# A hybrid mLSTM, Hyena and mixture-of-experts block on one core: its output projection in two passes, one half's chunks moved forward, and ring slots laid out anew

## The chip, the cores and the metric

The kernel runs on one core of one Trainium2 chip. The metric is the device time of one launch in microseconds (us). Before the change the median of three runs is 1379.07 us (1377.23 to 1380.62). The profiled execution, from which all rows below come, took 1378.79 us; its trace spans 1377.1 us.

## The reference

One encoder block on a sequence of 512 tokens, 1024 channels, in float32.

```
mod = c @ W_ada + b_ada                       # shift, scale, gate, twice
p   = (rms_norm(x) * (1 + sc1) + sh1) @ W_in  # q, k, v, o (4 heads x 128), gates, x1, x2, v of hyena
y_m = mlstm(q, k, v, o, gates)                # 4 heads, forward and backward, 512 channels
y_h = hyena(x1, x2, v)                        # 512 channels, two long convolutions by FFT
x   = x + gt1 * (concat(y_m, y_h) @ W_out)
hf  = rms_norm(x) * (1 + sc2) + sh2
aff = softmax(hf @ w_router)                  # 16 experts
g, idx = top_k(aff.T, 64)                     # each expert takes its 64 best tokens
x   = x + gt2 * sum over experts of silu(xs @ w_gate) * (xs @ w_up) @ w_down * g
out = rms_norm(x)
```

The weights of the experts are 16 x 3 matrices of 1024 x 2048 floats, 403 MB in all.

## The kernel before

**Stages.** First come the adaptive modulation (`w,par` matmuls on `in_w_ada`) and the spectra of Hyena's filters (`filters`, with DFT matmuls `s,d` on TensorE and complex products `H`, `j`, `k` on VectorE). Then `ORDER` lists the input projection in 512-channel parts and what follows each: `Z`, `X1`, `X2` are Hyena's parts, `C0` and `C1` its two long convolutions' forward sides, `I0` and `I1` the inverse ones, `K`, `Q`, `V`, `G`, `O` the mLSTM's parts, `H0` to `H3` its heads. The last large matmuls of this stage are those of `O`.

**Heads.** `stage(h, rows)` computes one head: four score matmuls (`x,y`), after each of which ScalarE and VectorE make weights `pt`; then `weighted` forms 20 sums (`j,pt`, 128x129) for the two directions. `head_out(h)` transposes the result and splits it into a high and a low part, the two halves `s` of `mixT[h]`. `cm_row` fetches a row for a head with a DMA on ScalarE's queue. `mixT[4]` to `mixT[7]` are Hyena's four chunks.

**Output projection.** `out_proj(i, q)` makes a tile of 128 tokens by 512 channels: 24 matmuls of 128x512 (8 chunks of three), Hyena's chunks first, then one VectorE multiply by `gt1` and one add into the residual `xt`. Eight such tiles are made in the order of `STEPS`. In this stage TensorE's order is pinned to program order (`pinned[0]`). Every finished tile starts a `turned` generator: transposes, the router's product, then, in `affinity`, the softmax, and at token tiles 1 and 3 `top64` (8 `MAX` and 7 `MATCH_REPLACE` on VectorE). `FOLLOW` says at which chunk of later tiles the generators take their next step.

**Weight ring.** The experts' matrices are read in 192 tiles of 2 MB on the SP queue, in order, into a ring of 8 slots. The ring's memory overlays that of the mixers, so each of its first 8 tiles waits until the mixer's slots under it are free. `SLOTS` gives the number of buffers of each tag.

VectorE, ScalarE and SP each run their instructions strictly in order. Elsewhere than in the pinned stage the order of an engine is that of the scheduler that builds the program.

## Time and profile before

| what | value |
|---|---|
| median of 3 runs | 1379.07 us (1377.23 to 1380.62) |
| profiled execution, its span | 1378.79 us, 1377.1 us |
| TensorE (PE) busy | 1277.3 us, 93% of the span |
| VectorE (DVE) busy | 514.8 us, 37% |
| ScalarE (ACT) busy | 259.4 us, 19% |
| read from memory | 460.53 MB, 338 GB/s over the span |

Times in rows are counted from the span's start. A row of the timeline gives the start, the duration, the engine and line, the operation with its output and input names, the shape and how many records are grouped. A float32 matmul that is no transpose shows as two records, one of kind fp32r and a transpose as one. The idle time ahead of an instruction and what ended it stand in brackets.

### The profile page before, as it was taken

To read this page: it belongs to the slowest core of one execution; us is meant where nothing else is said; L and a number is where in the kernel's file an instruction comes from. 1 tells how busy PE (TensorE), PEld (TensorE's weight loads), DVE (VectorE), ACT (ScalarE), POOL (GpSimd) and SP (SyncE) were. 2 spreads that over 40 slices of the span, in tenths; PEclk is the share of its full clock that TensorE was granted. 3 is DMA by queue.
4 is the path that set the end of the run, shared out by engine and by line. 5 is a ranking of instruction groups with operands and counts; after the bars stand their busy time and mean duration, and the time that the engine had idled before them with its cause. 6 is when DMAs were issued, how large, how long until landed. Compare 5 with 4: busy or idle time off the path is not lost.

```text
span 1377.1 us, 14496 instructions
## 1 busy us (share of the span) xinstructions
PE 1277.3 (93%) x5845; PEld 594.7 (43%) x5845; DVE 514.8 (37%) x1057; ACT 259.4 (19%) x561; POOL 32.4 (2%) x72
## 2 busy tenths in 40 slices
PE   4999999997896999999989998998999899899896
PEld 1466686674773334334333432433343243234332
DVE  5866796797663122221212212122121122212131
ACT  4523321456330101001010100101011010000111
POOL 0000000000000000000000000000000000000000
PEclk9999999999997999999999999999999999999999
DMA  9544444644109999999999999999999999999995
GB/s 350 181 169 140 151 154 136 198 144 169 61 20 408 393 430 425 427 426 427 428 426 426 426 425 427 430 426 425 427 425 427 428 426 426 427 426 427 428 406 214
DMA packets 58258, 466.06 MB, mean 338 GB/s; under 512 B 5448, under 2 KB 20040, under 8 KB 32464
## 3 DMA queue, kind: packets, MB, share of 16 engines
q1 hardware_dynamic: 53632, 455.56, 80.9%
q10 hardware_dynamic: 3216, 5.65, 1.3%
q0 software_dynamic: 1344, 3.94, 0.8%
q8 instruction: 46, 0.75, 0.2%
q14 instruction: 20, 0.16, 0.0%
HBM read 460.53 MB, written 4.60 MB: 338 GB/s over the span
## 4 chain that ended last, share of the span: by engine, by line
PE 72%; DMA 20%; DVE 3%; ACT 2%; issue 2%; POOLq 0%; SPq 0%; POOL 0%; DVEq 0%; ACTq 0%
PE ps L176 68%; DMA r<-in_w_up_dram 17%; PE ps L236 4%; DMA out_dram<-a 2%; DMA b<-in_hy_w_dram 1%; DMA w<-in_w_ada_dram 1%; DMA M<-cmd 1%; DVE M L1233 0%; ACT I L1232 0%; DVE M L990 0%; DVE M L992 0%; ACT jk L834 0%; ACT H L847 0%; ACT ps L268 0%; DVE a L1125 0%
## 5 line engine op out<-in xcount | busy, mean ns | idle before, releaser
L176 PE MATMUL ps<-r,x 128*64 128x512 f32 x2048 | 507.7, 616 | 34.0 <-DMA r<-in_w_up_dram 26.6
L176 PEld LDWEIGHTS ps<-r,x 128*64 128x64 f32 x2048 | 142.2, 140 | 305.6 <-issue 253.4
L176 PE MATMUL ps<-r,M 128*64 128x512 f32 x1024 | 232.0, 598 | 7.4 <-DVE M L1233 6.8
L1182 DVE SCALAR_TENSOR_TENSOR a<-ps,aff,a 128x512 f32<-128x512 f32 x120 | 90.1, 751 | 164.3 <-PE ps L176 164.3
L176 PEld LDWEIGHTS ps<-r,M 128*64 128x64 f32 x1024 | 69.3, 136 | 130.8 <-issue 118.0
L1222 DVE COPY I<-ps 128x512 f32<-128x512 f32 x32 | 22.1, 692 | 238.2 <-PE ps L176 222.1
L1224 ACT COPY I<-ps 128x512 f32<-128x512 f32 x32 | 18.7, 585 | 486.5 <-PE ps L176 486.5
L176 PE MATMUL ps<-a,l 128*128 128x512 f32 (+1 forms) x200 | 83.7, 418 | 0.0
L176 PE MATMUL ps<-a,h 128*128 128x512 f32 x192 | 81.0, 422 | 0.0
L1233 DVE TENSOR_TENSOR M<-ps,I 128x256 f32<-128x256 f32 x64 | 27.2, 424 | 141.4 <-ACT I L1232 139.7
L176 PE MATMUL ps<-b,h 128*128 128x512 f32 x192 | 79.9, 416 | 0.0
L176 PEld LDWEIGHTS ps<-M,h 128*128 128x128 f32 x512 | 63.3, 198 | 24.3 <-issue 17.0
L176 PE MATMUL ps<-M,h 128*128 128x128 f32 x512 | 68.9, 289 | 1.4 <-DVE M L1192 1.4
L176 PEld LDWEIGHTS ps<-V,H 128*128 128x128 f32 x120 | 22.3, 186 | 97.4 <-DVE a L1182 78.7
L176 PE MATMUL ps<-V,H 128*128 128x512 f32 x120 | 59.6, 497 | 0.0
L176 PE MATMUL ps<-s,d 128*128 128x512 f32 x112 | 56.5, 602 | 0.2 <-ACT H L361 0.2
L1232 ACT ACTIVATE I<-ps 128x256 f32<-128x256 f32 x64 | 24.5, 383 | 164.9 <-PE ps L236 164.9
L236 PEld LDWEIGHTS ps<-par,I 128*128 128x128 f32 x268 | 36.3, 208 | 40.8 <-issue 38.7
L1257 DVE TENSOR_TENSOR H<-ps,gt 128x512 f32<-128x512 f32 x15 | 10.4, 691 | 102.9 <-PE ps L176 102.9
L236 PE MATMUL ps<-par,I 128*128 128x128 f32 x268 | 45.8, 302 | 1.7 <-DVE I L1222 1.7
L176 PEld LDWEIGHTS ps<-a,h 128*128 128x128 f32 x192 | 36.1, 188 | 18.9 <-issue 9.6
L240 DVE TENSOR_TENSOR l<-w,h 128x1024 fp32r<-128x1024 f32 x32 | 38.1, 1219 | 16.4 <-ACT h L239 13.9
(313 smaller groups left out, 1148.9 us busy)
## 6 DMA issues: line engine op xcount, KB each, us to landing
r<-in_w_gate_dram SPq DMA_DIRECT2D x63, 2048.0 KB, 28.0
r<-in_w_up_dram SPq DMA_DIRECT2D x63, 2048.0 KB, 31.8
...
a<-in_w_ada_dram SPq DMA_DIRECT2D x2, 1024.0 KB, 15.1
...
```

What stands on the lines that cost most here:

```text
L176: return pin(pe.matmul(o, l, r, start=start, stop=stop))
L236: pin(pe.transpose(o, i, ident[0:k, 0:k]))
L240: dve.tensor_tensor(lo, v, hi.bitcast(F32), op=OP.subtract)
L1182: dve.scalar_tensor_tensor(xs, ps, aff[:, i, e:e + 1], xs, op0=OP.mult, op1=OP.add)
L1222: dve.tensor_copy(gs, gu[j])
L1224: act.copy(gs, gu[j])
L1232: act.activation(sg, pv[:, :, 0, :], AF.Silu)
L1233: dve.tensor_tensor(hidT[j // 2][:, j % 2 * 4:j % 2 * 4 + 4, :], pv[:, :, 1, :], sg, op=OP.mult)
L1257: dve.tensor_tensor(y, dn, gt2, op=OP.mult)
```

## The change

It does five things. `SLOTS` gives two of the four `s` buffers a tag `t` of their own, which the filters' sums, the spectra and Hyena's finished chunks use; the filter weights `w3` come in two halves, and four loads of `in_w_ada` go to other slots. `ORDER` puts `X1`, `I0` ahead of `K`, and `H0`, `H1` behind `I1`; `H3` is no longer in it. `out_proj` takes a list of chunks: it is called for chunks 4 to 7 of all eight tiles, and later for chunks 0 to 3 of all eight, and each call ends with the multiply and the add. The last head's `stage` yields after each score matmul and each `weighted`, and `WEAVE` takes its six pieces in between the eight first-pass tiles. `STEPS` has another order, and `FOLLOW` counts chunks over all tiles.

```diff
-SLOTS = {"h": 2, "a": 2, "x": 1, "l": 2, "s": 4, "j": 1, "k": 2, "b": 2, "y": 1, "d": 1}
+SLOTS = {"h": 2, "a": 2, "x": 1, "l": 2, "s": 2, "t": 2, "j": 1, "k": 2, "b": 2, "y": 1, "d": 1}
-ORDER = "Z C0 K Q X1 G I0 V C1 H0 H1 X2 I1 H2 O H3".split()
+ORDER = "Z C0 X1 I0 K C1 Q G V X2 I1 H0 H1 H2 O".split()
-STEPS = ((0, 0), (1, 0), (0, 1), (1, 1), (2, 0), (2, 1), (3, 0), (3, 1))
+STEPS = ((0, 0), (0, 1), (1, 0), (1, 1), (2, 0), (2, 1), (3, 0), (3, 1))
+WEAVE = (1, 1, 0, 0, 0, 1, 0, 1, 0, 1, 0, 1, 1, 1)
-FOLLOW = (3, 3, 5, 8, 1)
+FOLLOW = (3, 6, 8, 15, 16)
...
-            w3 = slot8("b")
-            for q in range(2):
-                sp.dma_start(w3[64 * q:64 * q + 64, :], a["hy_w3"][0])
+            w3 = [half(), half()]
+            for n in (1, 0):
+                for q in range(2):
+                    sp.dma_start(w3[n][64 * q:64 * q + 64, :], a["hy_w3"][0][:, n * 1024:(n + 1) * 1024])
...
-                plus, minus = q4(slot8("s")), q4(slot8("s"))
+                plus, minus = q4(slot8("t")), q4(slot8("t"))
...
-                    w = slot8("ab"[k // 2 % 2])
+                    w = slot8("ajak"[k // 2])
...
-            mixh, mixl = slot8("s", F32R), slot8("s", F32R)
+            mixh, mixl = slot8("t", F32R), slot8("t", F32R)
...
-        for q, g, t0 in ((0, 1, "h"), (0, 0, "h"), (1, 1, "x"), (1, 0, "y")):
+        for q, g, t0 in ((0, 1, "h"), (1, 1, "b"), (0, 0, "h"), (1, 0, "y")):
             wh = q4(slot8(t0, F32R))
-            wl = q4(slot8("jd"[g] if q else "l", F32R))
+            wl = q4(slot8("db"[g] if q else "l", F32R))
...
-        def out_proj(i, q):
+        def out_proj(i, q, ks):
+
             ps = bank("P")
             cs_ = slice(q * 512, (q + 1) * 512)
-            for n, k in enumerate((4, 5, 6, 7, 0, 1, 2, 3)):
-                yield n
-                mm3(ps, [t[:, i * 128:(i + 1) * 128] for t in mixT[k]], wo[q, k], start=(k == 4), stop=(k == 3))
+            for k in ks:
+                yield k
+                mm3(ps, [t[:, i * 128:(i + 1) * 128] for t in mixT[k]], wo[q, k], start=(k == ks[0]), stop=(k == ks[-1]))
...
-        early = [out_proj(*st) for st in STEPS[:EARLY]]
-        for g in early:
-            for n in g:
-                if n == 4:
-                    break
+
+        last_head = stage(3, [cm_row(6 + d) for d in range(2)])
+        hyenas = [out_proj(i, q, (4, 5, 6, 7)) for i, q in sorted(STEPS, key=lambda st: st[1])]
+        for n in WEAVE:
+            if n:
+                for _ in hyenas.pop(0):
+                    pass
+            else:
+                next(last_head)
         for h in range(3):
             head_out(h)
-        for g in early:
+        early = [out_proj(*st, (0, 1, 2, 3)) for st in STEPS[:EARLY]]
+        for m, g in enumerate(early):
+            if m == EARLY - 1:
+                head_out(3)
             for n in g:
-                if n == 7:
+                if n == 3:
                     break
-        head_out(3)
         for m, st in enumerate(STEPS):
-            for n in [7] if m < EARLY else out_proj(*st):
+            for n in [3] if m < EARLY else out_proj(*st, (0, 1, 2, 3)):
                 for t in todo:
-                    if t[1] and t[1][0] == n:
+                    if t[1] and t[1][0] <= 4 * m + n:
                         t[1].pop(0)
                         next(t[0], None)
...
-            todo.append((turned(*st), list(FOLLOW)))
+            todo.append((turned(*st), [4 * m + 4 + n for n in FOLLOW]))
```

**Place one: TensorE and VectorE behind the last DFT matmul of the filters.** Rows of the built program, with line, operation, output and input. On TensorE of the kernel before, behind the last `s,d` matmul, transposes of a first convolved part `V_650` stand ahead of 24 matmuls of the next part, and those of `V_686` and `V_749` behind them:

```order
L176 MATMUL ps_584<-s_481,d_81 128x512
L236 MATMUL ps_655<-par,V_650 128x128 x4
L176 MATMUL ps_949<-a_346,h_697 128x512
L176 MATMUL ps_949<-b_348,h_697 128x512
L176 MATMUL ps_949<-a_346,l_698 128x512
...
L236 MATMUL ps_691<-par,V_686 128x128 x4
L236 MATMUL ps_754<-par,V_749 128x128 x4
```

In the changed kernel the last DFT matmul is `t_484,d_84`, and the same transposes follow it (`V_653`, `V_689`, `V_752`):

```order
L178 MATMUL ps_587<-t_484,d_84 128x512
L178 MATMUL ps_710<-w_1002,par 32x512 x2
L178 MATMUL ps_710<-w_1003,par 32x512 x2
L239 MATMUL ps_658<-par,V_653 128x128 x4
L239 MATMUL ps_694<-par,V_689 128x128 x4
L239 MATMUL ps_757<-par,V_752 128x128 x4
L178 MATMUL ps_956<-a_349,h_700 128x512
```

The 24 projection matmuls now come behind the third group of transposes. On VectorE of the changed kernel this stands between that DFT matmul's result (`ps_587`) and `V_752`:

```order
L371 SCALAR_TENSOR_TENSOR H_593<-ps_587,H_591 128x512
L371 SCALAR_TENSOR_TENSOR H_591<-ps_587,H_591 128x512
L378 TENSOR_TENSOR j_544<-H_593,H_575 128x512 x2
L378 TENSOR_TENSOR j_544<-H_591,H_566 128x512 x2
L569 TENSOR_TENSOR V_752<-V_752,ecol 128x2
L569 TENSOR_TENSOR V_788<-V_788,ecol 128x2
L570 SCALAR_TENSOR_TENSOR V_752<-ps_727,vcol,V_752 128x511
L570 SCALAR_TENSOR_TENSOR V_788<-ps_763,vcol,V_788 128x511
L571 SCALAR_TENSOR_TENSOR V_752<-ps_727,vcol,V_752 128x511
```

In the kernel before these rows are the same, without the two of the second part (`V_788`) and with one of another part among them.

**Place two: TensorE between the last matmul of `O` and the first of the output projection.** Before, Hyena's transposes (`par,s`) and head 3 stand there:

```order
L236 MATMUL ps_2408<-par,s_2122 128x128 x4
L236 MATMUL ps_2417<-par,s_2122 128x128 x4
L176 MATMUL ps_2736<-j_1528,pt_2696 128x129 x3
L176 MATMUL ps_2741<-j_1528,pt_2696 128x129 x4
L176 MATMUL ps_2753<-j_1528,pt_2697 128x129 x4
L176 MATMUL ps_2759<-j_1528,pt_2697 128x129 x3
L176 MATMUL ps_2764<-j_1528,pt_2697 128x129 x2
L176 MATMUL ps_2768<-j_1528,pt_2697 128x129
L176 MATMUL ps_2807<-par,mod_598 128x16 x8
L176 MATMUL ps_2880<-h_2819,s_2388 128x512
```

In the changed kernel Hyena's transposes are followed by the last sums of head 1 (`pt_2324`) and then by all of head 2, and `h,t` is the first matmul of the projection:

```order
L239 MATMUL ps_2175<-par,s_1889 128x128 x4
L239 MATMUL ps_2184<-par,s_1889 128x128 x4
L178 MATMUL ps_2391<-j_1638,pt_2324 128x129 x2
L178 MATMUL ps_2395<-j_1638,pt_2324 128x129
L178 MATMUL ps_2443<-x_1378,y_1098 128x512
...
L178 MATMUL ps_2466<-x_1378,y_1098 128x512
L178 MATMUL ps_2474<-j_1638,pt_2441 128x129
...
L178 MATMUL ps_2513<-j_1638,pt_2442 128x129
L239 MATMUL ps_2571<-par,I_2565 128x128 x4
L178 MATMUL ps_2692<-par,mod_601 128x16 x8
L178 MATMUL ps_2777<-h_2704,t_2155 128x512
```

Head 3's four scores and 20 sums have moved from here into the first pass.

**Place three: VectorE at the end of the output projection.** `H_3327` (before) and `H_3334` (changed) are the product of the last tile with `gt1`; `MAX` of 16 rows is the first `top64`. Before, that `top64` ends ahead of the last tile's product:

```order
L990 MAX M_2878<-M_2878 16x8
L958 COPY M_2878<-M_2878 16x64
L971 SCALAR_TENSOR_TENSOR lg_3310<-ps_2877,rq_3293,lb 128x16
L973 TENSOR_REDUCE mx_3312<-lg_3310 128x1
L976 RECIPROCAL mx_3313<-mx_3313 128x1
L977 TENSOR_SCALAR aff<-aff,mx_3313 128x16
L907 TENSOR_TENSOR H_3327<-ps_3261,I_2864 128x512
...
L908 TENSOR_TENSOR a_2861<-a_2861,H_3327 128x512
...
L935 COPY V_3344<-ps_3339 128x256
...
L971 SCALAR_TENSOR_TENSOR lg_3370<-ps_2877,rq_3353,lb 128x16
```

In the changed kernel six of its seven `MATCH_REPLACE` stand behind the last tile's sum `a_2746`, and the copy `V_3379` and the logits `lg_3405` of the last token tile wait in line behind them:

```order
L916 TENSOR_TENSOR a_2746<-a_2746,H_3334 128x512
L981 TENSOR_REDUCE mx_3359<-lg_3357 128x1
L1000 MATCH_REPLACE M_2763<-M_2763 16x256
L998 MAX M_2763<-M_2763 16x8
...
L1000 MATCH_REPLACE M_2763<-M_2763 16x256
L943 COPY V_3379<-ps_3374 128x256
L998 MAX M_2763<-M_2763 16x8
L966 COPY M_2763<-M_2763 16x64
L979 SCALAR_TENSOR_TENSOR lg_3405<-ps_2762,rq_3388,lb 128x16
```

The first `top64` has moved from ahead of the last tile to behind it.

## Rows read from the trace of the kernel before

**Rows 1.** Busy time by stage (windows): window, its length, busy us (and instructions) of PE, PEld, DVE, ACT, POOL, the granted clock of TensorE, DMA share and GB/s.

```profile
100.00:150.00 50.00, 50.00 (x204) 31.58 (x203) 28.88 (x45) 19.05 (x27) 0.00 (x0) 1.00 0.47 148
316.99:351.30 34.31, 24.38 (x138) 17.40 (x136) 26.88 (x83) 25.69 (x87) 1.78 (x4) 0.90 0.38 139
351.30:409.98 58.68, 54.53 (x294) 42.32 (x294) 35.28 (x111) 17.70 (x45) 0.00 (x0) 1.00 0.10 37
409.98:427.87 17.89, 5.68 (x30) 4.78 (x29) 12.77 (x57) 2.75 (x7) 0.00 (x0) 0.58 0.97 392
478.00:1355.00 877.00, 839.17 (x3787) 315.16 (x3786) 192.43 (x334) 85.98 (x180) 13.46 (x33) 0.98 1.01 426
```

**Rows 2.** Timeline of TensorE around the last DFT matmul of the filters.

```profile
113.01 1.05 PE L176 MATMUL ps<-w,par 128*32 128x512 f32 x4
114.00 1.12 PE L176 MATMUL ps<-s,d 128*128 128x512 f32 x2
114.96 0.63 PE L236 MATMUL ps<-par,V 128*128 128x128 f32 x4
...
121.00 1.12 PE L236 MATMUL ps<-par,V 128*128 128x128 f32 x8
```

**Rows 3.** Timeline of VectorE in the same stretch.

```profile
115.24 0.69 DVE L367 SCALAR_TENSOR_TENSOR H<-ps,H 128x512 f32<-128x512 f32 x1 [0.92 <-PE ps L176]
...
117.04 1.28 DVE L374 TENSOR_TENSOR j<-H,H 128x512 f32<-128x512 f32 x2
...
118.32 1.28 DVE L374 TENSOR_TENSOR j<-H,H 128x512 f32<-128x512 f32 x2
...
120.30 0.75 DVE L567 SCALAR_TENSOR_TENSOR V<-ps,vcol,V 128x511 f32<-128x511 f32 x1
```

**Rows 4.** Timeline of TensorE from the last matmul of `O` (the first row) past the first (351.30) and the last matmul (409.59) of the output projection to the first expert's gather (427.87).

```profile
316.99 0.80 PE L176 MATMUL ps<-a,l 128*128 128x512 f32 x1
...
322.58 3.96 PE L176 MATMUL ps<-j,pt 128*128 128x129 f32 x34
...
326.87 2.74 PE L176 MATMUL ps<-x,y 128*128 128x512 f32 x6
337.45 2.49 PE L236 MATMUL ps<-par,s 128*128 128x128 f32 x8 [7.85 <-DVE s L838]
...
342.04 1.04 PE L236 MATMUL ps<-par,s 128*128 128x128 f32 x8
...
349.59 1.85 PE L176 MATMUL ps<-par,mod 128*128 128x16 f32 x16
351.30 0.48 PE L176 MATMUL ps<-h,s 128*128 128x512 f32 x1
...
359.40 0.39 PE L176 MATMUL ps<-x,s 128*128 128x512 f32 x1
...
409.59 0.39 PE L176 MATMUL ps<-y,s 128*128 128x512 f32 x1
...
427.87 0.58 PE L176 MATMUL ps<-M,h 128*128 128x128 f32 x1 [1.41 <-DVE M L1192]
```

**Rows 5.** Instructions grouped by line and shape, 317.6 to 428 us: line, engine, operation, out<-in, shapes, count, busy us, mean ns, idle before them.

```profile
L240 DVE TENSOR_TENSOR l<-w,h 128x1024 fp32r<-128x1024 f32 x2 | 2.4, 1217 | 0.0
...
L838 DVE TENSOR_TENSOR s<-s,zrs 128x512 f32<-128x512 f32 x4 | 2.5, 686 | 0.0
...
L848 DVE CAST s<-H 128x512 fp32r<-128x512 f32 x4 | 1.7, 424 | 0.7 <-ACT H L847 0.7
...
L907 DVE TENSOR_TENSOR H<-ps,I 128x512 f32<-128x512 f32 x8 | 5.5, 690 | 2.3 <-PE ps L176 2.2
```

**Rows 6.** Timeline of VectorE from the first `top64` to the last token tile's probabilities.

```profile
397.65 0.42 DVE L990 MAX8 M<-M 16x8 f32<-16x256 f32 x1
...
398.18 0.40 DVE L992 MATCH_REPLACE8 M<-M 16x256 f32<-16x256 f32 x1
...
407.84 0.42 DVE L990 MAX8 M<-M 16x8 f32<-16x256 f32 x1
...
415.03 0.23 DVE L971 SCALAR_TENSOR_TENSOR lg<-ps,rq,lb 128x16 f32<-128x16 f32 x1
...
416.62 0.23 DVE L977 TENSOR_SCALAR aff<-aff,mx 128x16 f32<-128x16 f32 x1
```

**Rows 7.** Timeline of the SP queue: issues of ring tiles.

```profile
321.00 0.46 SPq L1093 DMA_DIRECT2D r<-in_w_gate_dram  x1
370.38 0.34 SPq L1093 DMA_DIRECT2D r<-in_w_up_dram  x1
409.82 0.33 SPq L1093 DMA_DIRECT2D r<-in_w_gate_dram  x1
...
412.26 0.48 SPq L1093 DMA_DIRECT2D r<-in_w_up_dram  x1
440.91 11.45 SPq L1093 DMA_DIRECT2D r<-in_w_down_dram  x4
```

**Rows 8.** Windows of ten microseconds in the first expert; columns as in rows 1.

```profile
437.00:447.00 10.00, 9.22 (x47) 3.98 (x48) 0.18 (x1) 0.46 (x1) 0.00 (x0) 1.00 0.92 349
477.00:487.00 10.00, 10.00 (x52) 4.04 (x50) 0.85 (x2) 1.35 (x3) 0.00 (x0) 1.00 1.02 431
```

**Rows 9.** What TensorE waited for between 478 and 1355 us: us in all, times, the longest.

```profile
PE ps L176 <- DMA r<-in_w_up_dram: 26.6, 11, 3.8
```

More of the change, by code (lines that the diff above doesn't have):

```diff
@@ L305, in body @@
                 dve.tensor_tensor(hidp[lo, c], hid[hi, :], hidp[hi, c].bitcast(F32), op=OP.subtract)
-            w3h, w3l = slot8("s", F32R), slot8("l", F32R)
+            w3l, w3h = slot8("l", F32R), slot8("s", F32R)
             for b in (2, 3, 0, 1):
                 bs = slice(b * 512, (b + 1) * 512)
+                w = w3[b // 2][:, b % 2 * 512:b % 2 * 512 + 512]
                 with tc.issue_after(sins[W3A]):
-                    act.copy(w3h[:, bs], w3[:, bs])
-                dve.tensor_tensor(w3l[:, bs], w3[:, bs], w3h[:, bs].bitcast(F32), op=OP.subtract)
+                    act.copy(w3h[:, bs], w)
+                dve.tensor_tensor(w3l[:, bs], w, w3h[:, bs].bitcast(F32), op=OP.subtract)
         sel4 = slot8("h", F32R)
@@ L768, in stage @@
                     dve.scalar_tensor_tensor(v, ps[:, rg], SCALE, v, op0=OP.mult, op1=OP.mult)
+                yield
             for d in range(2):
                 weighted(h, d, pts[d])
+                yield
         def weighted(h, d, pt):
@@ L807, in head @@
         def head(h):
-            stage(h, [cm_row(2 * h + d) for d in range(2)])
+            for _ in stage(h, [cm_row(2 * h + d) for d in range(2)]):
+                pass
         def gated_1():
@@ L1021, in body @@
                 next(early[m], None)
-            for t in todo:
-                if t[1] and t[1][0] == 8 and m >= EARLY:
-                    t[1].pop(0)
-            todo.append((turned(*st), list(FOLLOW)))
+            todo.append((turned(*st), [4 * m + 4 + n for n in FOLLOW]))
         if dbg:
```

3 lines of the change are left out of this document (2 added, 1 removed).

## The prediction

> **What bounds the kernel now.** I read the stages first [rows 1]. From 478 to 1355 us the weights stream at 426 GB/s with a DMA share of 1.01, and TensorE waits there for arriving tiles, 26.6 us in all for one of the three matrices [rows 9]: the experts are a DMA stream. One tile of 2.097 MB takes 4.92 us at that rate. How that stream starts comes next [rows 7]. Two ring tiles are issued early, six in a row from 409.82 to 412.26, and the ninth only at 440.91, when TensorE frees a slot; around then the rate sinks to 349 GB/s and is back at 431 forty us later [rows 8]. So the ring is full before the first expert begins, and what starts the stream again is TensorE's work in that expert. The end of the kernel therefore follows the start of the first expert, 427.87 us [rows 4], nearly one for one. Ahead of that TensorE is the bound: between 100 and 150 us it is busy 50.00 of 50 [rows 1], so a hole made there lengthens the kernel. Only after the last matmul of the projection `O` (T0 = 316.99) is it idle: 9.9 of 34.3 us until the output projection starts at 351.30, 4.2 of 58.7 until the end of its last matmul, which starts at 409.59, and 12.2 of 17.9 until the gather [rows 1, 4].
>
> **How I worked.** I laid the instructions of the changed kernel, in the order of each engine, against durations from rows of before: each starts when the one ahead of it on its engine and the one it waits for are done. Prices on TensorE: a projection matmul 0.231 us (36 from 351.30 to 359.40), a weighted sum `j,pt` 0.233 (17 in 3.96), a score `x,y` 0.91 (3 in 2.74), a transpose 0.13 (8 in 1.04), a DFT matmul 0.96 (114.00 to 114.96) and a `w,par` matmul 0.5 (two from 113.01 to 114.00) [rows 2, 4]. On VectorE: 0.69 for 512 floats with about 0.08 of it overlapped, 0.42 for a cast, 1.22 for a split of a weight half [rows 5]. The same walk over the old order gives 32.2, 58.3 and 18.9 us for the three stretches where the trace has 34.3, 58.3 and 18.3, which is my measure of its error.
>
> **Before T0: +4.3 us.** By count, 17 weighted sums and 3 scores move from ahead of T0 to behind it and 4 DFT matmuls come ahead of it: -4.0 - 2.7 + 3.8 = -2.9 us. Against that stands a new hole at place one. Before, 5.5 us of projection matmuls lie between the transposes at 114.96 and those at 121.00, while VectorE works from 115.24 to 121.05 through two `H`, four `j` and two steps of `V` [rows 2, 3]. After, the transposes of the same `V` come right away: TensorE has four `w,par` matmuls (1.9 us) and eight transposes (1.0) beside a chain on VectorE of 6.1 + 0.7 us, since one step of the next part stands inside it too. The hole is 6.8 - 2.9 = 3.9 us. Smaller holes come out at the start of the first projection (a PSUM bank that VectorE frees, about 0.9) and at three later places (0.7 to 1.0 each); I take 3.3 for all, with 0 and 5 as ends. The sum is +4.3. The halved `w3`, the four moved loads and the tag `t` cost nothing: they lie in the start-up, which waits for other things; without that cover a load of 0.5 MB costs 1.2 us at 426 GB/s.
>
> **T0 to the first projection matmul: 34.3 becomes 26.7.** VectorE is what TensorE waits for. Behind T0 it still has four products with `zrs` (2.4, of which 0.9 lie ahead of T0), four weight splits (4.6), eight casts and subtractions of Hyena's halves (3.8), three steps of head 1 (1.9), seven pieces of `pt` (2.8), `k` and small ones (2.0): 16.6 us until the bank of head 2's last score is free, 16.2 in the walk. Then TensorE does that score, 20 sums, four transposes and the modulation's products (1.85): 8.0, and 1.5 of waits for ScalarE's copies; 25.7 in all. Before, the 7.85 us wait at 337.45 was followed by slow work: eight transposes took 2.49 us, at 342.04 again 1.04, and the clock granted over the whole stretch was 0.90 [rows 1, 4]. After, there is a wait of about 5.7 us ahead of that last score. I add 1.0 us for work at the lower clock (ends 0 and 2.3). Gain: 7.6 us.
>
> **The two passes: 58.3 becomes 66.9.** The 192 matmuls stay: 44.4 us. Head 3 has come in: four scores 3.6 and 20 sums 4.7, so pass one lasts 22.2 + 8.3 + 1.5 (12 transposes) = 32.0. At the seam the first `s` halves wait for VectorE and ScalarE as before, 0.3 us more. The eight additional products and sums are 16 x 0.69 = 11 us on VectorE; they cost nothing, since pass one gives it 32 us for some 25 us of work, and would cost a bank wait of 0.7 us each without that. Loss: 8.6 us.
>
> **The end: 18.3 becomes 23.6.** Before, the first `top64` ran from 397.65 to 408.26, ahead of the last matmul, and the last token's probabilities came at 416.62 [rows 6]. `FOLLOW` now lets token tile 1 finish at step 4 x 3 + 4 + 16 = 32, and the last step is 31, so the first `MAX` starts some 1.2 us ahead of the last matmul. What VectorE must do until the last token's logits is 8 x 0.45 + 7 x 0.52 us of `top64` and 5 us of other steps in line, 12.2 in all, which ends 11.0 us behind the last matmul; the softmax takes 1.3 more. The probabilities come 12.3 us after it, not 7.0 (409.59 to 416.62). Queued behind are the second `top64`, the slots and the gather. Loss: 5.3 us, nearly sure, as VectorE runs in order.
>
> **The ring: -1 us.** Five tiles instead of two can load before the last matmul: the second slot is freed by the last matmul of pass one, three by `head_out(3)`. But the ring was already full when the first expert began to free slots; by 477 us some 0.2 of a tile more has landed: 1.0 us. The far end is three tiles, 14.7 us.
>
> **Sum:** 4.3 - 7.6 + 8.6 + 5.3 - 1.0 = +9.6. On the profiled execution's 1378.79 us, 0.28 below the median, that gives 1388.4 us.
>
> **The rivals.** *The weave fills the idle time.* From T0 to the last matmul TensorE is busy 24.4 + 54.5 = 78.9 of 93.0 us [rows 1]. If pass one starts as soon as Hyena's halves are there and the sums of head 3 fill every hole, 14.1 us go instead of the 1.0 that I add there: 1388.4 - 15.1 = 1373.3 us. For it: the holes are real, and VectorE is idle in the middle of them. Against it: all of head 2 stands ahead of pass one in TensorE's order (place two), and its last score waits for VectorE. It decides at a start of pass one about 13 us behind T0, where the walk has those halves ready. Chance 0.13. The Trainium skill, "Perfetto Trace Analysis", section Optimization Strategy, says that a kernel whose most contended engine changes over time may be improved by interleaving those regimes; that is what the weave is, and by it this rival would be the likeliest; the trace agrees with its premise by the idle 14.1 us, and no run here shows yet what follows from it.
>
> *The ring's start sets the end.* Then three tiles more ahead of the experts take 14.7 us off instead of 1: 1374.7, not slower. For it: the share is 1.01 from 478 on. Against it: the dip to 349 GB/s and the issue at 440.91, which waits for TensorE [rows 7, 8]. It would need slots freed before the first expert runs. Chance 0.04.
>
> *The late terms cancel.* If the hole at place one is covered (VectorE further ahead than in the trace) and the smaller ones as well, 4 to 7 us go; if the last token's logits were not held up, 5.3. One gives 1381 to 1384, both 1376 to 1379: no measurable change. Chance 0.16.
>
> *More half-clock work.* If the wait ahead of pass one puts its first 30 matmuls at the lower clock, they take 7 us more: above 1394. Against it: only 1.5 us of waiting directly precede them. Chance 0.06.
>
> **The numbers.** Chances: forecast, 1383 to 1394, 0.61; the rivals 0.13, 0.04, 0.16, 0.06. A measurement of this kernel tells about 0.3%, 4 us, from no change: slower is above 1383.2, faster below 1374.9. So slower 0.67, same 0.16, faster 0.17. The range reaches down to about the first two rivals' times and up to the end of the forecast's, 1374 to 1394; what it leaves out is the fourth rival and the better half of the first. The forecast's own range is 1383 to 1394.
>
> **What would show it.** A hole of about 4 us on TensorE near 119, ended by a step of `V` on VectorE; T0 near 321; the first `h,t` matmul about 27 us later; the last `y,s` near 415; no 16x256 `MAX` more than 2 us ahead of it; the probabilities some 12 us behind; the gather near 438; five ring tiles issued before the last matmul, and a rate of 0 GB/s for a while between the eighth tile's landing and the first freed slot. I am wrong if the hole near 119 is missing, if pass one starts within 20 us of T0, or if the end doesn't follow the gather.

## The result and the profile after

The changed kernel takes 1392.35 us (median of 4 runs, 1391.20 to 1394.16) beside 1379.82 us before on the same chip: a ratio of 1.0098 with a 95% interval of 1.0086 to 1.0109. It is slower: the medians are 12.5 us apart, and by the ratio it is 13.5. The forecast was 1388.4 us, and slower. The profiled execution took 1394.16 us with a span of 1392.5, 15.4 us more span than before. Where they went is read at the same places as before:

| us, profiled executions | before | forecast | after |
|---|---|---|---|
| first matmul of `Z` | 73.13 | no change | 75.97 (+2.8) |
| last matmul of `O` (T0) | 316.99 | +4.3 | 325.60 (+8.6) |
| T0 to first projection matmul | 34.3 | 26.7 | 26.6 (-7.7) |
| first to last projection matmul | 58.3 | 66.9 | 66.7 (+8.4) |
| last projection matmul to gather | 18.3 | 23.6 | 24.6 (+6.3) |
| gather to the end of the span | 949.2 | -1.0 | 949.0 (-0.2) |

The rows of after that answer to [rows 1], in the same columns; the first is a stretch of the start-up and has its row of before right behind it.

```profile
30.00:40.00 10.00, 7.71 (x31) 2.32 (x34) 6.14 (x10) 1.33 (x2) 0.00 (x0) 0.83 0.85 313
100.00:150.00 50.00, 46.09 (x189) 31.17 (x188) 23.71 (x35) 14.46 (x20) 0.00 (x0) 0.97 0.32 103
325.60:352.20 26.60, 19.41 (x122) 15.97 (x121) 20.16 (x56) 16.87 (x48) 1.82 (x4) 0.81 0.35 112
352.20:418.88 66.68, 62.03 (x339) 47.75 (x339) 45.49 (x126) 26.66 (x76) 1.27 (x2) 1.00 0.43 165
418.88:443.46 24.58, 7.44 (x32) 6.16 (x31) 19.99 (x84) 4.53 (x11) 0.00 (x0) 0.58 0.64 256
```

```profile
30.00:40.00 10.00, 10.00 (x42) 3.00 (x41) 7.29 (x13) 2.31 (x4) 0.00 (x0) 1.00 0.94 356
```

TensorE was busy all of 30 to 40 us and all of 100 to 150 us before; after, it lacks 2.29 us in the one and 3.91 in the other. The stretch of the two passes is well filled (62.0 of 66.7), the tail behind it is not (7.4 of 24.6). The timeline of TensorE of after names the waits; the bracket gives the idle time ahead of a row and what ended it.

```profile
33.52 2.28 PE L178 MATMUL ps<-w,par 128*32 128x512 f32 x6 [2.29 <-DMA w<-in_w_ada_dram]
...
75.97 0.50 PE L178 MATMUL ps<-a,h 128*128 128x512 f32 x1 [1.08 <-DVE M L406]
...
116.43 1.30 PE L239 MATMUL ps<-par,V 128*128 128x128 f32 x8
121.65 0.72 PE L239 MATMUL ps<-par,V 128*128 128x128 f32 x4 [3.92 <-DVE V L571]
122.12 0.67 PE L178 MATMUL ps<-a,h 128*128 128x512 f32 x1
...
125.58 0.44 PE L178 MATMUL ps<-a,l 128*128 128x512 f32 x1
...
341.85 2.08 PE L178 MATMUL ps<-x,y 128*128 128x512 f32 x2 [6.67 <-DVE pt L772]
...
432.58 0.38 PE L239 MATMUL ps<-par,aff 128*16 128x128 f32 x1 [1.43 <-DVE aff L985]
439.86 0.26 PE L239 MATMUL ps<-par,mx 16*128 16x16 f32 x1 [6.89 <-DVE mx L1050]
...
443.46 2.08 PE L178 MATMUL ps<-M,h 128*128 128x128 f32 x8 [1.41 <-DVE M L1203]
```

And the SP queue of after, which answers to [rows 7]: the second pair of `w` tiles of `w_ada` and the two pairs behind it in the start-up, then the first and the fifth tile of the ring.

```profile
17.17 19.85 SPq L439 DMA_DIRECT2D w<-in_w_ada_dram  x6
...
368.50 0.34 SPq L1104 DMA_DIRECT2D r<-in_w_gate_dram  x1
...
392.72 0.42 SPq L1104 DMA_DIRECT2D r<-in_w_gate_dram  x1
```

### The profile page after: what moved, and what is told of

Same layout as the page of the kernel before. It is cut to its first block, busy times and chain, and to the rows that moved or that the text cites. A ratio compares the mean times of both kernels' runs of the same rounds, so it can differ in the third digit from the quotient of the medians.

```text
span 1392.5 us, 14525 instructions
## 1 busy us (share of the span) xinstructions
PE 1279.6 (92%) x5845; PEld 608.3 (44%) x5845; DVE 524.0 (38%) x1073; ACT 260.9 (19%) x561; POOL 29.9 (2%) x72
## 4 chain that ended last, share of the span: by engine, by line
PE 73%; DMA 19%; DVE 4%; issue 2%; ACT 1%; SPq 0%; POOLq 0%; POOL 0%; ACTq 0%; DVEq 0%
PE ps L178 70%; DMA r<-in_w_up_dram 14%; PE ps L239 4%; DMA w<-in_w_ada_dram 2%; DMA out_dram<-a 2%; DMA M<-cmd 1%; DMA w<-in_hy_w_dram 1%; DVE M L1000 0%; DVE M L1244 0%; DVE M L998 0%; ACT I L1243 0%; DVE a L1136 0%; DVE H L915 0%; DVE a L916 0%; DVE H L371 0%
## 5 line engine op out<-in xcount | busy, mean ns | idle before, releaser
L178 PEld LDWEIGHTS ps<-r,x 128*64 128x64 f32 x2048 | 152.3, 139 | 294.2 <-issue 229.7
L178 PEld LDWEIGHTS ps<-r,M 128*64 128x64 f32 x1024 | 69.5, 136 | 132.1 <-issue 119.5
L1233 DVE COPY I<-ps 128x512 f32<-128x512 f32 x32 | 22.1, 691 | 242.5 <-PE ps L178 226.3
L178 PEld LDWEIGHTS ps<-M,h 128*128 128x128 f32 x512 | 63.3, 198 | 24.3 <-issue 17.0
L1243 ACT ACTIVATE I<-ps 128x256 f32<-128x256 f32 x64 | 24.5, 383 | 164.9 <-PE ps L239 164.9
L1118 DVE TENSOR_SCALAR x<-ps,A,mod 128x128 f32<-128x128 f32 x32 | 13.1, 410 | 94.2 <-PE ps L178 94.2
L178 PE MATMUL ps<-w,par 128*32 128x512 f32 x160 | 33.7, 650 | 15.2 <-ACT ps L271 9.3
L243 DVE TENSOR_TENSOR l<-w,h 128x1024 fp32r<-128x1024 f32 x32 | 38.4, 1219 | 17.0 <-ACT h L242 15.4
```

Of the source, the lines that this page charges most:

```text
L178: return pin(pe.matmul(o, l, r, start=start, stop=stop))
L243: dve.tensor_tensor(lo, v, hi.bitcast(F32), op=OP.subtract)
L1118: dve.tensor_scalar(xsT[:, k, :], v, A2[:, k:k + 1], mod2[:, 0, k:k + 1], op0=OP.mult, op1=OP.add)
L1233: dve.tensor_copy(gs, gu[j])
L1243: act.activation(sg, pv[:, :, 0, :], AF.Silu)
```

## The experiments

Twelve kernels were run. The times are compared as ratios to the kernel before on the same chip, with 95% intervals; the places come from each one's timeline (one profiled execution each, in us; T0 is the last matmul of `O`, P the projection's matmuls).

| kernel | first `Z` | T0 | T0 to first P | first to last P | last P to gather | gather to end | ratio |
|---|---|---|---|---|---|---|---|
| before | 73.13 | 316.99 | 34.3 | 58.3 | 18.3 | 949.2 | 1 |
| after | 75.97 | 325.60 | 26.6 | 66.7 | 24.6 | 949.0 | 1.0098 (1.0086 to 1.0109) |
| e_w3 | 73.61 | 323.80 | 23.8 | 68.1 | 24.6 | 949.0 | 1.0083 (1.0065 to 1.0100) |
| e_ordc | 75.81 | 327.36 | 26.1 | 68.3 | 24.3 | 949.5 | 1.0138 (1.0116 to 1.0161) |
| e_order | 75.70 | 322.41 | 26.1 | 69.7 | 24.6 | 948.8 | 1.0099 (1.0082 to 1.0117) |
| e_tag | 75.28 | 327.64 | 24.5 | 66.7 | 24.6 | 948.2 | 1.0102 (1.0084 to 1.0120) |
| e_ordtt | 74.53 | 318.65 | 23.0 | 69.5 | 24.3 | 950.6 | 1.0070 (1.0058 to 1.0082) |
| e_both | 76.67 | 330.03 | 12.7 | 77.1 | 24.0 | 948.6 | 1.0066 (1.0051 to 1.0081) |
| e_top1 | 76.95 | 328.15 | 24.0 | 68.3 | 22.1 | 950.0 | 1.0078 (1.0061 to 1.0095) |
| b_pass | 73.77 | 317.63 | 22.2 | 69.9 | 24.0 | 947.7 | 1.0045 (1.0030 to 1.0060) |
| e_onepass | 75.18 | 325.09 | 39.8 | 58.4 | 18.3 | 948.2 | 1.0101 (1.0086 to 1.0115) |
| e_slots | 76.48 | 326.65 | 24.2 | 68.5 | 24.6 | 948.5 | 1.0102 (1.0087 to 1.0118) |
| e_best | 73.69 | 317.29 | 19.2 | 75.8 | 19.8 | 948.3 | 1.0027 (1.0018 to 1.0036) |
| b_slots | 72.62 | 316.48 | 27.9 | 58.4 | 18.3 | 950.1 | 0.9963 (0.9949 to 0.9977) |

A place in one execution is no median. After, e_onepass and e_top1 have the same code ahead of T0, and T0 lies at 325.60, 325.09 and 328.15, so a difference of 3 us there tells nothing by itself.

### The halves of the change: b_pass and e_onepass

**The passes alone.** From the changed kernel, everything ahead of the projection goes back to what it was:

```diff
-ORDER = "Z C0 X1 I0 K C1 Q G V X2 I1 H0 H1 H2 O".split()
+ORDER = "Z C0 K Q X1 G I0 V C1 H0 H1 X2 I1 H2 O".split()
...
-            w3 = [half(), half()]
...
+            w3b = slot8("b")
...
-        for q, g, t0 in ((0, 1, "h"), (1, 1, "b"), (0, 0, "h"), (1, 0, "y")):
+        for q, g, t0 in ((0, 1, "h"), (0, 0, "h"), (1, 1, "x"), (1, 0, "y")):
...
```

> The two passes alone: the changed kernel with its start-up, its tags and slots (w3, t, the w_ada loads, w_out's slots) and its ORDER as in the kernel before, so that only the split output projection, the weave of head 3, STEPS and FOLLOW are left of the change. Theory 'two losses' (start-up and hole ahead of O's last matmul; the last token's logits behind the last matmul): first Z matmul and O's last matmul as before (73.1 and 317 within 1 us), no wait near 121, the stretch behind the last matmul still 24 us in place of 18.3, and the time 4 to 7 us above before, about 1384 where before is 1378.7. Rival 'the passes are the whole loss': 10 to 13 us above before. A third: the weave pays, within 3 us of before.

Measured: 4.7 us above before by the medians (1383.5 beside 1378.85), 6.2 by the ratio. `Z` and T0 are within 0.7 us of before, TensorE waits for nothing near 121, and the tail is 24.0. The theory of two losses holds for this half. Between T0 and the last projection matmul the passes are about even (92.1 us, before 92.6); their cost is the tail, 5.7 us.

**All but the passes.** The changed kernel with the old loop around a one-pass `out_proj`:

```diff
-ORDER = "Z C0 X1 I0 K C1 Q G V X2 I1 H0 H1 H2 O".split()
+ORDER = "Z C0 X1 I0 K C1 Q G V X2 I1 H0 H1 H2 O H3".split()
...
-            for k in ks:
+            for n, k in enumerate((4, 5, 6, 7, 0, 1, 2, 3)):
...
```

> The counterpart: the changed kernel with the output projection in one pass, H3 in ORDER, STEPS and FOLLOW as before; the start-up, tags, slots and the order of Hyena's chunks as changed. Theory 'the order of the chunks pays only with the weave': O's last matmul at 325 to 326 as in the changed kernel, the last matmul to the gather back at 18 to 19, but 34 to 40 us from O's last matmul to the first projection matmul, so that the gather comes at 438 to 443 and the time is 10 to 13 us above before, about that of the changed kernel. Rival 'the passes are the loss': 3 to 6 us above before.

Measured: 13.3 us above before (0.3 above the range), as much as the whole change, with all three places as the first theory has them: T0 325.09, 39.8 us to the projection, 18.28 to the gather, which is before's 18.28 to the hundredth. So the two halves don't add up: 4.7 and 13.3 alone, 12.5 together. What the new order pushes behind T0, the two passes with the weave of head 3 in part take back: from T0 to the last projection matmul e_onepass has 98.2 us, the changed kernel 93.3, before 92.6.

### Ahead of T0: e_w3, e_ordc, e_tag, e_order, e_ordtt

**The halved `w3`.**

```diff
-            w3 = [half(), half()]
-            for n in (1, 0):
-                for q in range(2):
-                    sp.dma_start(w3[n][64 * q:64 * q + 64, :], a["hy_w3"][0][:, n * 1024:(n + 1) * 1024])
+            w3b = slot8("b")
+            for q in range(2):
+                sp.dma_start(w3b[64 * q:64 * q + 64, :], a["hy_w3"][0])
+            w3 = [w3b[:, 0:1024], w3b[:, 1024:2048]]
```

> The changed kernel with the halved w3 alone undone: w3 is again one tile in the b slot and no longer holds two of the four w buffers. Theory 'start-up': the third pair of w_ada tiles is issued sooner, TensorE's wait near 33 us goes, the first matmul of Z comes 2.3 to 2.9 us earlier than the changed kernel's 75.97, and the time falls by 2.3 to 3 us, to about 1389.5. Rival 'the other start-up edits' (four loads put into other slots, the tag t, the changed order of the queue): the wait stays, the time changes by less than 0.7 us.

Measured: the first `Z` matmul at 73.61, 2.36 us sooner, and the gather 3.2 us sooner than in the changed kernel. SP's queue in e_w3, then TensorE's row:

```profile
8.23 3.31 SPq L439 DMA_DIRECT2D w<-in_w_ada_dram  x2
```

```profile
73.61 0.50 PE L178 MATMUL ps<-a,h 128*128 128x512 f32 x1 [1.10 <-DVE M L406]
```

The second pair of `w_ada` tiles is issued at 8.23 us; in the changed kernel it stands in a row of six that begins at 17.17, because the halves of `w3` hold two of the four `w` buffers, and TensorE waits 2.29 us for it. That wait is gone in e_w3. (The expectation calls this pair the third.) The step is shown by the trace; by the ratio alone (1.0083 and 1.0098, overlapping intervals) it would not be. The other executions agree: in the nine that have the halves the first `Z` matmul comes at 74.53 to 76.95 us, in the five that don't at 72.62 to 73.77.

**The hole at place one.** Four kernels, in this order. e_ordc moves one phase:

```diff
-ORDER = "Z C0 X1 I0 K C1 Q G V X2 I1 H0 H1 H2 O".split()
+ORDER = "Z C0 K X1 I0 C1 Q G V X2 I1 H0 H1 H2 O".split()
```

> The changed kernel with K moved in ORDER from behind I0 to ahead of X1, so that other matmuls stand again between the filters' last DFT matmul and the transposes of the same V. Theory 'hole': the 3.92 us wait at 121.65 shrinks below 1 us, O's last matmul comes 3.5 to 5 us earlier than 325.60, and the gather and the end follow by as much: about 1388. Rival 'VectorE is the bound there': the wait comes back at a later place of the same stretch, and O's last matmul and the time change by less than 1 us.

Measured: the hole theory fails, and its rival is right in kind only. The wait moved by one group: eight transposes run, then the first matmul of `K` waits for VectorE's step of `V` in their place. T0 is 1.8 us later than in the changed kernel, which is within the scatter. The time is 19.4 us above before, 7 us more than the changed kernel's; the six runs reach from 1392.05 to 1401.99 us, the profiled execution is only 3.1 us longer than that of after, and where the rest goes stays open. e_tag and e_order then undo one part each, e_ordtt both:

```diff
-SLOTS = {"h": 2, "a": 2, "x": 1, "l": 2, "s": 2, "t": 2, "j": 1, "k": 2, "b": 2, "y": 1, "d": 1}
+SLOTS = {"h": 2, "a": 2, "x": 1, "l": 2, "s": 4, "j": 1, "k": 2, "b": 2, "y": 1, "d": 1}
...
-                plus, minus = q4(slot8("t")), q4(slot8("t"))
+                plus, minus = q4(slot8("s")), q4(slot8("s"))
...
-ORDER = "Z C0 X1 I0 K C1 Q G V X2 I1 H0 H1 H2 O".split()
+ORDER = "Z C0 K Q X1 G I0 V C1 H0 H1 X2 I1 H2 O".split()
```

> The changed kernel with ORDER as before (without H3) and the tag t merged back into s (four s tiles, as before); the halved w3, the w_ada loads and w_out's slots stay as changed. The build of this kernel puts four V transposes behind the filters' last DFT matmul and the next eight 24 matmuls later, as before; with K moved alone eight transposes stayed together and the wait stayed too. Theory 'order and tag make the hole together': no wait over 1 us between 110 and 135, O's last matmul 5 to 8 us earlier than 325.60, the time 4 to 8 us below the changed kernel's, 1384 to 1388. Rival 'VectorE bounds that stretch': O's last matmul stays at 324 or later.

> The changed kernel with the tag t alone merged back into s (four s tiles); ORDER as changed. In this build twelve V transposes still stand together behind the filters' last DFT matmul. Theory 'the order of TensorE's rows makes the hole': a wait of 3.5 to 4 us for V near 120 as in the changed kernel, O's last matmul at 324 to 327, the time within 3 us of the changed kernel's. Rival 'the tag makes it': no wait over 1 us there, O's last matmul 4 us sooner.

> The changed kernel with ORDER as before (without H3) and the tag t kept. In this build eight V transposes stand together behind the filters' last DFT matmul, and the projection matmuls behind them need a bank that VectorE frees. Theory 'order and tag make the hole together': a wait of 2.5 to 3.5 us near 120 that stands on a matmul in place of a transpose, O's last matmul 2 to 4 us later than the 318.65 of the kernel with both undone. Rival 'the order alone makes it': no wait over 1 us there and O's last matmul within 1 us of 318.65.

TensorE's timeline at that place, in turn e_ordc, e_tag, e_order and e_ordtt:

```profile
116.72 1.23 PE L239 MATMUL ps<-par,V 128*128 128x128 f32 x8
120.70 0.47 PE L178 MATMUL ps<-a,h 128*128 128x512 f32 x1 [2.76 <-DVE V L569]
```

```profile
122.64 1.10 PE L239 MATMUL ps<-par,V 128*128 128x128 f32 x4 [3.26 <-DVE V L571]
```

```profile
120.59 0.47 PE L178 MATMUL ps<-a,h 128*128 128x512 f32 x1 [3.14 <-DVE V L569]
```

```profile
116.75 0.75 PE L239 MATMUL ps<-par,V 128*128 128x128 f32 x4 [0.45 <-ACT H L365]
...
122.87 1.12 PE L239 MATMUL ps<-par,V 128*128 128x128 f32 x8
```

With only one part undone a wait of 3 us stays (in e_tag 3.26 us, and T0 at 327.64, both just outside what was expected), and so does the time (1.0102 and 1.0099). With both undone four transposes run, matmuls fill the next 5.4 us, the other eight follow without a wait, and T0 is 318.65, 7 us sooner in these two executions; the time falls to 1.0070, which is 3.9 us by the ratios. So each of the two makes a hole without the other, `ORDER` in e_tag and the tag `t` in e_order, and each hides the other: to undo one shows nothing. All nine kernels that have the changed `ORDER` (e_both without `H2`, e_ordc with `K` moved) or the tag `t` wait there, 2.76 to 3.92 us. In before, e_ordtt, b_pass and b_slots, which have neither, no wait reaches 0.5 us, and none does in e_best, which has the tag undone and `K` and `Q` ahead of `X1`. The hole costs more than its 3.9 us, as the windows of the changed kernel ahead of the hole, behind it and further on show (length, busy us of TensorE, granted clock, DMA share, GB/s):

```profile
116.40:121.60 5.20, 1.33 (x10) 1.00 0.65 203
121.70:125.50 3.80, 3.80 (x12) 0.57 0.00 0
125.90:127.60 1.70, 1.70 (x9) 1.00 0.00 0
```

Behind the wait the granted clock is 0.57: the eight projection matmuls from 122.12 to 125.58 take 0.43 us each, and 0.23 from then on. That is 1.6 us more.

### Between T0 and the passes: e_both

Head 2 leaves `ORDER` and is woven like head 3:

```diff
-ORDER = "Z C0 X1 I0 K C1 Q G V X2 I1 H0 H1 H2 O".split()
+ORDER = "Z C0 X1 I0 K C1 Q G V X2 I1 H0 H1 O".split()
...
-WEAVE = (1, 1, 0, 0, 0, 1, 0, 1, 0, 1, 0, 1, 1, 1)
+WEAVE = (0, 0, 1, 1, 0, 1, 0, 0, 0, 0, 1, 0, 0, 1, 0, 1, 0, 1, 0, 1)
...
-        last_head = stage(3, [cm_row(6 + d) for d in range(2)])
+        def last_heads():
+            for h in (2, 3):
+                yield from stage(h, [cm_row(2 * h + d) for d in range(2)])
+
+        last_head = last_heads()
```

> The changed kernel with head 2 woven into pass one as well (H2 leaves ORDER, and its steps stand between those of pass one as head 3's do). Theory 'place two' (head 2 ahead of pass one in TensorE's order is what keeps the weave from filling the idle time): pass one starts about 13 us behind O's last matmul in place of 26.6, the wait of 6.7 us near 342 goes, the last projection matmul comes 4 to 8 us sooner, and the time falls by 4 to 8 us, to 1384 to 1388. Rival 'VectorE owes the same work': pass one starts earlier but waits for VectorE inside, the last matmul and the time change by less than 2 us.

Measured: pass one starts 12.7 us behind T0, as expected, and the wait of 6.67 us is gone. The windows of e_both from T0 to the first and to the last projection matmul:

```profile
330.03:342.71 12.68, 11.76 (x79) 9.77 (x77) 12.10 (x29) 9.21 (x19) 1.24 (x3) 0.85 0.54 198
342.71:419.81 77.10, 71.98 (x383) 55.09 (x382) 53.45 (x153) 34.21 (x105) 2.22 (x3) 0.96 0.39 147
```

TensorE idles 6.0 us there in place of 11.8, but from T0 to the last matmul the gain is 3.5 us (89.8 for 93.3), short of the 4 to 8 that were expected: it is busy for 83.7 us in place of 81.4, with a granted clock of 0.96 in the passes where after has 1.00. T0 itself comes later in this execution, where the granted clock was 0.91 from 60 to 100 us and 0.89 from 125 to 150 (after: 1.00 and 0.99), so the ratio, 4.4 us under the changed kernel's, is the better measure of the whole. Place two was the obstacle that the prediction named; with it gone the weave is worth some 4 us, not 15.

### The tail: e_top1

One sorted list for each half of the tokens, made in one go behind the last token, in place of two lists of which the first stands alone:

```diff
-                if i == 1:
-                    top64(top0, w0)
-                    dve.tensor_copy(w1[0:16, 0:64], top0)
-                elif i == 3:
-                    top64(top2, w1[0:48, 0:160])
+                if i == 3:
+                    top64(top2, w1[0:48, 0:256])
...
```

> The changed kernel with one sorted list per half of the tokens made in a single top64 over 48 partitions x 256, so that the separate first top64 (15 instructions on VectorE) is gone and the last one's MATCH_REPLACE are 256 wide instead of 160. Theory 'VectorE in order': without the first list the last token's logits come 2.5 to 5 us sooner behind the last matmul (14.0 to 16 in place of the last 12.3 + 6.3 split), the longer last list costs 0.8 back, so the stretch from the last matmul to the gather falls from 24.6 by 2 to 4 us: about 1389.5. Rival 'the other engines' chain': ScalarE's copies and TensorE's transposes of the last token set the end, the first list only filled VectorE's waits; then the longer last list makes it 0.8 to 1.5 us slower: about 1393.5.

TensorE in e_top1: last projection matmul, last token's probabilities, end of the sorted list, gather.

```profile
420.38 0.40 PE L178 MATMUL ps<-y,s 128*128 128x512 f32 x1
...
430.09 0.38 PE L239 MATMUL ps<-par,aff 128*16 128x128 f32 x1 [1.43 <-DVE aff L982]
438.77 0.28 PE L239 MATMUL ps<-par,mx 16*128 16x16 f32 x1 [8.30 <-DVE mx L1046]
...
442.50 1.83 PE L178 MATMUL ps<-M,h 128*128 128x128 f32 x7 [1.50 <-DVE M L1199]
```

The transpose of the last probabilities comes 9.7 us behind the last matmul, in the changed kernel 13.7 (432.58 - 418.88); the list takes 1.4 us more (a wait of 8.30 for 6.89). The tail is 2.5 us shorter, and the first theory holds: VectorE's first list in line was what held the last token. The time alone (1.0078, overlapping intervals) doesn't tell e_top1 from the changed kernel. With the list gone the tail is still 3.8 us above before's. Of these, 1.4 are the longer last list. The other 2.3 lie ahead of the transpose of the last probabilities, where other tokens' steps stand in TensorE's order ahead of the last token's transposes. e_best, which also puts those transposes first, has the transpose 7.4 us behind its last matmul (412.34), as before has it (409.59), and a tail of 19.8. The row of e_best, then that of before:

```profile
419.72 0.38 PE L241 MATMUL ps<-par,aff 128*16 128x128 f32 x1 [1.84 <-DVE aff L984]
```

```profile
417.00 0.37 PE L236 MATMUL ps<-par,aff 128*16 128x128 f32 x1 [2.01 <-DVE aff L977]
```

### The slots: e_slots and b_slots

Both change only the places of `w_out`, e_slots back in the changed kernel, b_slots forward in the kernel before:

```diff
-        for q, g, t0 in ((0, 1, "h"), (0, 0, "h"), (1, 1, "x"), (1, 0, "y")):
+        for q, g, t0 in ((0, 1, "h"), (1, 1, "b"), (0, 0, "h"), (1, 0, "y")):
             wh = q4(slot8(t0, F32R))
-            wl = q4(slot8("jd"[g] if q else "l", F32R))
+            wl = q4(slot8("db"[g] if q else "l", F32R))
```

> The changed kernel with only the places of w_out undone: (q 0, heads) second, x, y, j and d as before. Then only two ring tiles can be issued before the last projection matmul, in place of five. Theory 'the ring was full anyway': from the gather to the end 948.5 to 950 as with five, the time within 3 us of the changed kernel's or a little less, since the first projection matmul comes some 2 us sooner by the order of VectorE's splits. Rival 'the early tiles pay': three tiles fewer, the stretch from the gather to the end grows by up to 14.7 us, the time is 1395 or more.

> The kernel before with only the places of w_out changed, as in the change: the group (q 1, Hyena) goes second and to slots b and d in place of x and j, its other half to b. Theory 'the placement works through TensorE's order': with those loads and splits at another time the eight transposes behind head 2's last score no longer wait 7.85 us for VectorE's products with zrs, O's last matmul stays at 317, the first projection matmul comes 3 to 5 us sooner than 351.30, and so do the gather and the end: 1374 to 1376 where before is 1378.8. Theory 'the ring' (more tiles ahead of the experts pay by themselves): the stretch from the gather to the end falls below 949 by several us. Rival 'nothing hangs on the places': within 1.5 us of before.

Measured: e_slots is not told from the changed kernel (1.0102 and 1.0098); three ring tiles, not two, are issued ahead of its last matmul. b_slots is 4.9 us faster than before and the fastest of all. The first ring tile on its SP queue, and then TensorE:

```profile
400.23 0.34 SPq L1093 DMA_DIRECT2D r<-in_w_gate_dram  x1
```

```profile
332.72 2.08 PE L176 MATMUL ps<-x,y 128*128 128x512 f32 x2 [3.49 <-DVE pt L768]
...
344.40 0.48 PE L176 MATMUL ps<-h,s 128*128 128x512 f32 x1
```

No ring tile at all is issued before 400 us, and the stretch from the gather to the end is 950.1 all the same. With five early tiles (after) it is 949.0, with three (e_slots) 948.5, with two 949.2 (before) and 947.7 (b_pass): in no order of their number, so the early tiles are worth nothing that these executions show, and the rival of 14.7 us falls. The theory of TensorE's order has the direction, but not the size: the eight transposes wait for nothing, the score that now stands ahead of them waits 3.49 us for `pt`, and the first projection matmul comes 6.9 us sooner, not 3 to 5.

What b_slots gains lies between T0 and the projection, 27.9 for 34.3 us. ScalarE shows it. `M<-cmd` is a small load, 0.26 MB, that a head's weights `pt` need. First before, with the ring tile issued at 321.00 [rows 7] on its way; then b_slots; then the changed kernel, with loads of `x` and `w_out` on their way:

```profile
325.60 0.33 ACTq L741 DMA_DIRECT2D M<-cmd  x1
...
332.83 0.62 ACT L766 ACTIVATE pt<-M,gcol 128x384 f32<-128x384 f32 x1 [5.74 <-DMA M<-cmd]
```

```profile
324.85 0.33 ACTq L741 DMA_DIRECT2D M<-cmd  x1
...
328.08 1.31 ACT L766 ACTIVATE pt<-M,gcol 128x384 f32<-128x384 f32 x3 [0.88 <-DMA M<-cmd]
```

```profile
329.46 0.33 ACTq L745 DMA_DIRECT2D M<-cmd  x1
...
336.78 0.61 ACT L770 ACTIVATE pt<-M,gcol 128x384 f32<-128x384 f32 x1 [3.23 <-DMA M<-cmd]
```

From issue to the first use it takes 3.2 us in b_slots and 7.2 and 7.3 in the others. In the windows of before and of b_slots at that time the DMA share is 0.99 and 0.44:

```profile
327.00:329.00 2.00, 2.00 (x6) 0.82 (x5) 2.00 (x13) 0.09 (x1) 0.29 (x1) 1.00 0.99 426
```

```profile
327.00:329.00 2.00, 2.00 (x6) 0.68 (x4) 1.97 (x11) 1.12 (x4) 1.11 (x2) 1.00 0.44 145
```

The packets say which transfer moved. The first row is the only one of before from 325.6 to 329.1, the first 3.5 us behind the issue; the others are of b_slots for as long behind its issue, with a second load `M<-cmd` in it (queue, kind: packets, MB, share of 16 engines; q1 is the queue of SP's loads, q10 that of `M<-cmd`):

```profile
q1 hardware_dynamic: 143, 1.53, 102.7%
```

```profile
q10 hardware_dynamic: 195, 0.37, 40.8%
q1 hardware_dynamic: 10, 0.02, 1.4%
```

So in before the small load, issued at 325.60, had not moved a packet 3.5 us later. A 2 MB tile that nobody needs for 100 us, the last of 4.2 MB issued on SP's queue from 317.82 on, held up a 0.26 MB load that TensorE needed at once, through ScalarE and VectorE. The Trainium skill, "SBUF — State Buffer", section "The DMA setup-cost knee", gives about 2 us plus the bytes at 436 GB/s for one transfer: an estimate of 2.6 us for this one, near the 3.2 of b_slots; the 4 us more are not in it.

It need not be a ring tile: in after it is `x` and `w_out`. Six kernels have the changed kernel's steps between T0 and the projection, and the stretch goes with this load: 26.6 us in after (7.3 from issue to use), 26.1 in e_ordc (6.1), and 23.8 to 24.5 in e_w3, e_slots, e_top1 and e_tag (5.2 to 5.5). A part of that, up to 1.0 us, is the clock: TensorE is busy for 19.4 us of the stretch in after and for 18.4 to 18.9 in the last four. It also fits that the same edit does nothing in the changed kernel: there the first ring tile is issued at 368.50 us with it and at 375.49 without (e_slots). How much of the 6.4 us in b_slots is the load's is an estimate, up to 4.0 (7.2 - 3.2): the edit also moves eight transposes behind head 2's last score in TensorE's order, and the one was not tried without the other.

### All together: e_best

`w3` in one tile, `s` as before, `ORDER` "Z C0 K Q X1 I0 C1 G V X2 I1 H0 H1 O", both heads woven as in e_both, one list as in e_top1, `FOLLOW` counted from the first chunk of a tile in place of the last for the first three tiles, and ahead of the last loop

```diff
+        next(todo[7][0], None)
+        next(todo[5][0], None)
+        next(todo[6][0], None)
+        next(todo[7][0], None)
         for t in todo:
             for _ in t[0]:
                 pass
```

> What the theories add up to: w3 in one tile, the tag s as before, ORDER 'Z C0 K Q X1 I0 C1 G V X2 I1 H0 H1 O', heads 2 and 3 both woven into pass one, one top64 over 48 x 256, and the last token's transposes ahead of the other tokens' last steps. Start-up 2.4 and T0 5 to 10 us sooner than the changed kernel, first projection matmul about 20 us behind O's last, last matmul near 408 to 411, 20.5 us from there to the gather: 428 to 432, so the time is 0 to 4 us above before, 1378 to 1383. If VectorE's work behind O's last matmul is more than the rows say, the wait moves into pass one and it is 1386 or more.

Measured: 3.3 us above before (1.0027, interval 1.0018 to 1.0036); T0 317.29, the last matmul at 412.34, 19.8 us from there to the gather. Each part shows at its place, and together they take back 9 of the 12.5 us. They don't quite add: by the ratios it is 9.8 us, where e_w3, e_ordtt, e_both and e_top1 alone give back 13.1. A version in two passes that beats the kernel before was not found. One edit of the change alone, b_slots, does beat it.

## Why the prediction came out as it did

**The time** fell into the forecast's own range, 4 us above the forecast. Of its five terms the first was short by half, and the second came out by errors that cancel. The end follows the gather as said: 947.7 to 950.6 us behind it in all fourteen kernels.

**Before T0: the mis-sized term**, +8.6 for +4.3. The step that failed is "The halved `w3`, the four moved loads and the tag `t` cost nothing: they lie in the start-up". The halves of `w3` put off a pair of loads that TensorE waits for: 2.8 us up to `Z`, of which e_w3 gives back 2.4 (the four moved loads were not tried alone). The bound of 1.2 us without cover was too low, since I priced a load and not the buffer that it waits for. The tag `t` is alone enough for a hole of 3 us at place one (e_order), far behind the start-up; it cost nothing more only because the new `ORDER` makes that hole too (e_tag). The size of that hole, 3.9 us, was right (3.92), and so was VectorE's step of `V` as what ends it; its after-effect, 1.6 us at a granted clock of 0.57, was not in the sum. The 2.8 and the 1.6 us make up the 4.3 that the sum lacks; its smaller holes were not read one by one. e_ordtt, without the hole, has 244.1 us from `Z` to T0, before 243.9, after 249.6.

**T0 to the first projection matmul**: 26.6 for 26.7, in part by luck. The last score starts 16.25 us behind T0 (341.85), where the walk has 16.2. But VectorE is busy for 13.05 of them, not for 16.6: it stands idle twice ahead of the score, 3.2 us in all, for ScalarE's `pt`, which waits for `M<-cmd`. VectorE's rows of after:

```profile
338.41 1.15 DVE L772 SCALAR_TENSOR_TENSOR pt<-ps,pt 128x512 f32<-128x512 f32 x2 [2.20 <-ACT pt L768]
...
341.50 0.72 DVE L772 SCALAR_TENSOR_TENSOR pt<-ps,pt 128x128 f32<-128x128 f32 x2 [1.00 <-ACT pt L768]
```

I took the wait of 7.85 us in [rows 4] for VectorE's own work and did not ask what VectorE had waited for. Its row of before says it, 5.12 us for the same `pt`:

```profile
334.46 0.69 DVE L768 SCALAR_TENSOR_TENSOR pt<-ps,pt 128x512 f32<-128x512 f32 x1 [5.12 <-ACT pt L764]
```

After, a wait of 6.67 us stands where 5.7 was forecast; the transfer behind it was missed. From the score to the projection two errors cancel again, 10.4 us for 10.5. The 1.5 us of waits for ScalarE's copies are not there, and the work priced at 8.0 takes 2.4 us more, not 1.0, since the granted clock is 0.54 from the score on (columns as in [rows 1]):

```profile
341.85:348.00 6.15, 6.15 (x24) 5.12 (x25) 4.10 (x17) 2.80 (x14) 0.00 (x0) 0.54 0.00 0
```

In e_w3 and e_top1, where the load took 5.3 and 5.5 us, the same stretch takes 23.8 and 24.0 us.

**The two passes**: 66.7 for 66.9, with no bank waits from the eight additional products, as said. The sum is at full clock, and so is after's execution; in e_w3 and e_ordc, at a granted clock of 0.97, the same passes take 68.1 and 68.3 us.

**The end**: 24.6 for 23.6. The probabilities of the last token come 13.4 us behind the last matmul (forecast 12.3), and the first `MAX` 0.2 us ahead of it (forecast 1.2). VectorE's rows of after, which answer to [rows 6]:

```profile
418.64 0.42 DVE L998 MAX8 M<-M 16x8 f32<-16x256 f32 x1
...
430.09 0.42 DVE L998 MAX8 M<-M 16x8 f32<-16x256 f32 x1
...
432.29 0.23 DVE L985 TENSOR_SCALAR aff<-aff,mx 128x16 f32<-128x16 f32 x1
```

"Nearly sure, as VectorE runs in order" held: e_onepass has before's 18.28 us back. But the list is the larger part and not the whole: without it the last probabilities still come 2.3 us later than before, behind other tokens' steps on TensorE (e_top1, e_best), which the sum doesn't have as a term of their own.

**The ring**: -0.2 for -1.0, nothing that a measurement tells; right in kind, and b_slots shows it with no tile before 400 us. What the slots really did was elsewhere, at the small load, and was not seen.

**The rivals.** The weave's point of decision was put at 13 us behind T0. e_both reaches it and wins about 4 us, so the rival's price of 15.1 was wrong too: it counted all idle time as to be had, and 6.0 us are idle in e_both. By the sentence that the prediction took from the Trainium skill, "Perfetto Trace Analysis", section Optimization Strategy, interleaving the regimes may improve such a kernel; the runs agree in direction (e_both idles less and is 4.4 us faster than the changed kernel); it paid for less than the new order cost. Of the late terms that might cancel, neither the hole nor the wait of the last token's logits did. More half-clock work came, but ahead of T0 (0.57) and on head 2's last score and sums (0.54), not in pass one (the granted clock over both passes is 1.00).
